# Last output tile in two passes over half the tokens, y laid out by halves, and 18 instead of 12 first products

## The chip, the cores and the metric

The kernel runs on one core of a Trainium2 chip. The metric is the device time of one execution in microseconds, from the median of the runs shown. The engines are called as in the profile: PE is TensorE's products, PEld its weight loads (they overlap the products), DVE is VectorE, ACT ScalarE, POOL GpSimd, SP SyncE, which here only issues DMAs.

## The reference, cut to what matters

One inference step of a hybrid decoder with two layers, for 256 prompt tokens and 8 sample tokens, model width 1024, f32. Each layer is a mixer with residual, then a feed-forward part with residual:

```python
def conv_ffn(x, prev, norm_g, w_gate, w_up, conv_w, conv_b, w_down):
    T = x.shape[1]
    h = rmsnorm(x, norm_g)
    g = h @ w_gate
    g_all = jnp.concatenate([prev, g], axis=1)
    gc = sum(conv_w[i] * g_all[:, i:i + T] for i in range(CONV_W)) + conv_b
    a = jax.nn.gelu(gc) * (h @ w_up)
    return x + a @ w_down, g_all[:, -(CONV_W - 1):]
...
y_prompt = rmsnorm(xp, final_norm)
y_sample = rmsnorm(xs, final_norm)
```

The change sits at the very end: `a @ w_down` of layer 1 (2816 to 1024), the residual, and the final RMSNorm, which needs the sum of squares over all 1024 channels of a token before any channel of that token can be scaled. It also touches the very beginning, where products of ones keep TensorE busy until the first data arrive.

## The kernel before, in words

All 264 tokens are columns: activations lie with 128 channels on the partitions and the T = 264 tokens along the row. X, the residual stream, is a tile of 128 x 8 x 264, one slice m of 264 columns for each 128 channels.

Weights are packed on the host into blocks of 128 x 128 in exactly the order in which TensorE uses them. They come from memory in chunks of 8 or 16 blocks (`raw`, issued on SP's queue), and `split` turns 8 blocks at a time into a high part `wh` (ScalarE, L299, rounded to fp32r) and a low part `wl` (VectorE, L300, the remainder). Activations have the same two parts. A block therefore costs three products, all with a moving operand of 128 x 264: high weights times high activations, high times low, low times high, each with a weight load of its own. `run` goes over an order of (output tile m, block k), adds into one PSUM bank for each m, and calls `evac(m, o)` after the last block of m. In the down projection `dn1` there are 8 output tiles of 22 blocks (NF = 22), 66 products each.

`residual(..., operand=False, R=R)` gives the evac of `dn1`: z = PSUM times R of the feed-forward norm (L579), X += z (L581), the square of X (`Norm.add`, L397 on ScalarE; the squares of tiles 0 to 6 are summed into `acc_fin` on GpSimd, that of tile 7 stays apart), and X times the gain of the final norm (L586). `Norm.finish` then multiplies `acc_fin` and the last square by a matrix of ones on TensorE (`ns_fin`, ordinary fp32, two rows in the profile for each product), which sums over the partitions; Ln and Exp on ScalarE (L421, L422) make `R_fin`. The last loop (L1093 to L1096) scales X in five pieces on VectorE and stores each, on SP's and ScalarE's queue in turn:

```python
    for i, (m, e) in enumerate(YD):
        x = X[:, m:e, :]
        v.tensor_tensor(x, x, R.unsqueeze(1).to_broadcast([P, e - m, T]), ALU.mult)
        (s if i % 2 else nc.sync).dma_start(a["y"][m:e].rearrange("m p t -> p m t"), x)
```

At the beginning, WARM = 12 bf16 products of a tile of ones (128 x 256, `warm`) run before the first real product (L372, L373).

The order on each engine is made by a scheduler when the program is built, except where `keep_in_program_order` pins it: `fixed[0]` pins TensorE's products in the mixers, and the weight DMAs are pinned on SP.

Of the kernel before, what the change touches and what calls it, by code (L numbers as in the profile page):

```python
# [9 lines left out]
F32 = mybir.dt.float32  # L10
# [3 lines left out]
AF = mybir.ActivationFunctionType  # L14
ALU = mybir.AluOpType
# [3 lines left out]
P = 128  # L19
D = 1024  # L20
KD = D // P
SEQ = 256
NS = 8
T = SEQ + NS
# [7 lines left out]
NF = DFF // P  # L32
# [2 lines left out]

MMB = 4
KQ = 5
WARM = 12
YD = ((0, 1), (1, 3), (3, 5), (5, 7), (7, 8))

NEG = -1e30
SCALE = HD ** -0.5
# [108 lines left out]
def _consts():  # L151
# [41 lines left out]
    ("sguw", (P, 512)), ("sgub", (P, 512)), ("poolw", (P, 512)),  # L193
]
_OUTS = [
    ("y", (KD, P, T)), ("k0", (P, 4, T)), ("v0", (P, 4, T)), ("bvn", (P, 4, NS)),
    ("k1", (P, 4, T)), ("v1", (P, 4, T)), ("poolp", (P, 4, NST)), ("pools", (P, 4, NS, 16)),
    ("cv0", (P, NF, 10)), ("cv1", (P, NF, 10)), ("cs0", (P, NF, NS)), ("cs1", (P, NF, NS)),
]
# [3 lines left out]
def tile_decoder_step(ctx: ExitStack, tc: tile.TileContext, a):  # L203
    nc = tc.nc
    v, s, g = nc.vector, nc.scalar, nc.gpsimd
    fixed = [False]
# [13 lines left out]
    pe = TensorE()  # L220
# [6 lines left out]
    sm = ctx.enter_context(tc.tile_pool(name="sm", bufs=3))  # L227
# [3 lines left out]
    def f4(name, shape=(P, 4, T), dt=F32):  # L231
        return up.tile(list(shape), dt, tag="u", name=name)

    def mv(name):
        return [f4(f"{name}_{x}", dt=F32R) for x in "hl"]

    def hl(tiles, k):
        return tiles[k // 4][0][:, k % 4, :], tiles[k // 4][1][:, k % 4, :]

    def at(name):  # L240
        return psa.tile([P, 512], F32, tag="at", name=name)

    X = con.tile([P, KD, T], F32, name="X")
# [7 lines left out]
    def mmb(name):  # L251

        return psm.tile([P, 512], F32, tag="mm", name=name)

    def vec(n):
        o, w = _VEC[n]
        return VEC[:, o:o + w]
# [18 lines left out]
    def wtiles(tt):  # L276
        return [wsp.tile([P, 8 * P], F32R, tag=f"w{x}", name=f"w{x}{tt}") for x in "hl"]

    def raw(ci):
        if ci not in raws:  # L280
            n = _CHUNKS[ci] * P
            r = f4(f"raw{ci}", (P, n)) if ci < C8 else rawp.tile([P, n], F32, tag="raw", name=f"raw{ci}")
            o = (coff[ci] - 16) * P * P
            raws[ci] = r
            late(r, a["w"][o:o + P * n].rearrange("(p f) -> p f", p=P))
        return raws[ci]

    LOOK = 3
    pos = [0]

    def split(t):
        for tt in range(len(splits), min(t + (2 if t == 3 else LOOK), NT - 1) + 1):
            ci = chunk_of[tt]
            for c in range(ci, min(ci + 3, len(_CHUNKS))):
                raw(c)
            o = (tt * 8 - coff[ci]) * P
            src = raws[ci][:, o:o + 8 * P]
            h, l = splits[tt] = wtiles(tt)
            s.activation(h, src, AF.Copy)  # L299
            v.tensor_tensor(l, src, h.bitcast(F32), ALU.subtract)  # L300
        return splits[t]

    spare = (32, 40)

    def run(order, rhs, evac, hooks=None):
        hooks = sorted((hooks or {}).items())
        n = 0
        seen, left, ps = {}, {}, {}
        for m, k in order:
            left[m] = left.get(m, 0) + 1  # L310
        for m, k in order:
            i = pos[0]
            pos[0] += 1
            h, l = split(i // 8)
            c = (i % 8) * P
            if m not in ps:
                ps[m] = at(f"mm{i}") if i in spare else psm.tile([P, 512], F32, tag="mm", name=f"mm{i}")
                first = True
            else:
                first = False  # L320
            left[m] -= 1
            o = ps[m][:, :T]
            xh, xl = rhs(m, k)
            pe.matmul(o, h[:, c:c + P], xh, start=first, stop=False)
            pe.matmul(o, h[:, c:c + P], xl, start=False, stop=False)
            pe.matmul(o, l[:, c:c + P], xh, start=False, stop=left[m] == 0)
            if left[m] == 0:
                evac(m, o)
            n += 1
            while hooks and n >= round(8 * (hooks[0][0] + 1)):  # L330
                for f in hooks.pop(0)[1]:
                    f()

    orders = dict(_PHASES)
# [9 lines left out]
    first, o = [], 0  # L344
    for i in range(len(_FIRST)):
        g_, w_, x_ = _first_cols(i)
        n = g_ + w_ + x_
        r = f4(f"xw{i}", (P, n))
# [22 lines left out]
    pw = at("warm")  # L371
    for i in range(WARM):  # L372
        tc.keep_in_program_order(pe.matmul(pw[:, :256], warm[:, :P], warm, start=i == 0, stop=i == WARM - 1))  # L373

    ident = cst("ident")
    ones = con.tile([P, P], F32, name="ones")
    v.memset(ones, 1.0)
    epst = con.tile([P, 1], F32, name="epst")
# [11 lines left out]
    class Norm:  # L390
        def __init__(self, name, two=False):
            self.name, self.two, self.last = name, two, []
            self.acc = None

        def add(self, m, src=None):
            q = sm.tile([P, T], F32, tag="sq", name=f"sq_{self.name}{m}")
            i = s.activation(q, X[:, m, :] if src is None else src, AF.Square)  # L397
            if src is not None:
                tc.keep_in_program_order(i)
            if m == KD - 1 and self.two:  # L400
                self.last.append(q)
            elif self.acc is None:
                self.acc = q
            elif m == 1:
                n = sm.tile([P, T], F32, tag="acc", name=f"acc_{self.name}", bufs=2)
                g.tensor_tensor(n, self.acc, q, ALU.add)
                self.acc = n
            else:
                g.tensor_tensor(self.acc, self.acc, q, ALU.add)
# [1 line left out]
        def finish(self, pin=False):  # L411
            return rstd_of([self.acc] + self.last, 1.0 / D, self.name, pin)

    def rstd_of(parts, scale, name, pin=False, bank=None):
        p = (bank or at)(f"ns_{name}")
        for i, x in enumerate(parts):
            mm = pe.matmul(p[:, :T], ones, x, start=i == 0, stop=i == len(parts) - 1)
            if pin:
                tc.keep_in_program_order(mm)
        R = sm.tile([P, T], F32, tag="R", name=f"R_{name}", bufs=2)  # L420
        s.activation(R, p[:, :T], AF.Ln, bias=epst, scale=scale)  # L421
        last[0] = s.activation(R, R, AF.Exp, scale=-0.5)  # L422
        return R

# [111 lines left out]
        g.tensor_tensor(C0[:, l], C0[:, l], t, ALU.add)  # L536
        nc.sync.dma_start(a[f"cs{l}"], CSTATE[:, l, 1])

    def ffn(l, xg, R, down_evac, hooks=None):
        cw, cb = vec("cw"), vec("cb")  # L540
        wc = lambda i, j: cw[:, (l * 3 + i) * NF + j:(l * 3 + i) * NF + j + 1]
        cvo = sm.tile([P, NF, 10], F32, tag="cvo", name=f"cvo{l}", bufs=1)
        act = [mv(f"a{l}_{i}") for i in range((NF + 3) // 4)]
        half = {}

        def evac(m, o):
            n, j = m
            if n == "g":
                wk = f4(f"wk{l}_{j}", (P, 2, T))
                C = wk[:, 0, :]  # L550
                G = wk[:, 1, :]
                v.tensor_tensor(G, o, R, ALU.mult)  # L552
                s.activation(C, G, AF.Identity, scale=wc(2, j), bias=cb[:, l * NF + j:l * NF + j + 1])
                v.scalar_tensor_tensor(C[:, 1:SEQ], G[:, 0:SEQ - 1], wc(1, j), C[:, 1:SEQ], ALU.mult, ALU.add)
                v.scalar_tensor_tensor(C[:, 2:SEQ], G[:, 0:SEQ - 2], wc(0, j), C[:, 2:SEQ], ALU.mult, ALU.add)
                v.tensor_tensor(C[:, SEQ:T], C[:, SEQ:T], C0[:, l, j, :], ALU.add)
                s.activation(cvo[:, j, :], G[:, SEQ - 2:T], AF.Copy)
                s.activation(C, C, AF.Gelu_apprx_tanh)
                half[j] = wk
            else:  # L560
                wk = half.pop(j)
                C, A = wk[:, 0, :], wk[:, 1, :]
                v.tensor_tensor(A, o, C, ALU.mult)
                halves(*hl(act, j), A)

        run(orders[f"ff{l}"], lambda m, k: hl(xg, k), evac)
        nc.sync.dma_start(a[f"cv{l}"], cvo)
        lnexp()
        run(orders[f"dn{l}"], lambda m, k: hl(act, k), down_evac, hooks)

    def residual(gain, name, operand=True, R=None):
        xg = [mv(f"xg_{name}{i}") for i in range(2)] if operand else None
# [23 lines left out]
    xg = [mv(f"xg_0{i}") for i in range(2)]  # L596
    nrm = Norm("n0", True)
# [307 lines left out]
    xg, nrm, evac = residual(vec("f0"), "f0")  # L905
    run(orders["out0"], pick([catA, catB]), evac, hk)
    fixed[0] = False
    R = nrm.finish()
    gelu_set()
    xg1, nrm1, evac = residual(vec("n1"), "n1", R=R)  # L910
# [9 lines left out]
    xg = xg1  # L920
# [164 lines left out]
    xg, nrm, evac = residual(vec("f1"), "f1")  # L1085
    run(orders["out1"], pick([catA, catB]), evac, hk)
    fixed[0] = False
    R = nrm.finish()
    gelu_set()
    _, nrm, evac = residual(vec("fin"), "fin", operand=False, R=R)  # L1090
    ffn(1, xg, R, evac)
    R = nrm.finish()
    for i, (m, e) in enumerate(YD):  # L1093
        x = X[:, m:e, :]
        v.tensor_tensor(x, x, R.unsqueeze(1).to_broadcast([P, e - m, T]), ALU.mult)  # L1095
        (s if i % 2 else nc.sync).dma_start(a["y"][m:e].rearrange("m p t -> p m t"), x)  # L1096


def _lay(inp):
# [66 lines left out]
```

## Time and profile before

| what | value |
|---|---|
| median of 3 runs | 603.81 us (603.23 to 604.20) |
| the profiled execution, device time | 605.38 us |
| its span in the profile | 603.6 us |
| granted TensorE clock over the span | 0.997 |
| PE, DVE, ACT busy | 590.4, 424.7, 339.9 us |
| last product of the last output tile starts | 593.72 us |
| last y scaling ends | 599.85 us |

The span lacks the 1.8 us that lie around it in the device time. In the timeline a row is: start in us, length in us, engine, line, operation, output from inputs, shapes, how many instructions were merged into the row, and in brackets the idle time of the engine before it with what ended it. In groups, the numbers behind the bar are total us and mean ns of one instruction. A product's length includes a drain that overlaps the next product, so a stream's cost is read from start to start. "a" is the feed-forward activation (high and low part), "mm" a PSUM accumulator of the trunk, "half" in the changed kernel one of half the tokens.

### The profile page before, as it was taken

Reading aid. Unit: us, or ns where it says so; the run is one execution under the profiler, and the core shown is the slowest. Engines: PE = TensorE matmul, PEld = TensorE weight load, DVE = VectorE, ACT = ScalarE, POOL = GpSimd, SP = SyncE. Lnnn points to the kernel's source line nnn. Section 1 sums busy time; section 2 is a strip of 40 time slices with the busy share of each in tenths; the row PEclk is TensorE's granted clock in tenths of the full one; section 3 lists DMA queues with packets and bytes.
Section 4 is the critical chain, followed back from the end, with each engine's and each line's share of the span. In section 5 each row is a group of like instructions: output and inputs, shape, how many; then the busy total and the mean of one; then the engine's idle time right before and its main releaser. Section 6 shows DMA issues by size and latency. Waiting matters only on the chain.

```text
span 603.6 us, 12258 instructions
## 1 busy us (share of the span) xinstructions
PE 590.4 (98%) x4900; PEld 571.4 (95%) x4900; DVE 424.7 (70%) x745; ACT 339.9 (56%) x597; POOL 42.8 (7%) x59
## 2 busy tenths in 40 slices
PE   8989999999999999999999999999999999999994
PEld 7988879999999999999999878999999999999993
DVE  6899565958878778576569676686877777755542
ACT  7557754656555656454454466656665555555431
POOL 4101002300000000001120000030000000001210
PEclk9999999999999999999999999999999999999998
DMA  8998845454554645796466763554545545455402
GB/s 310 352 378 328 272 153 205 155 204 149 201 176 174 208 150 201 260 370 212 151 251 248 262 206 113 173 205 148 208 149 201 179 171 207 152 208 171 179 1 72
DMA packets 28090, 122.39 MB, mean 203 GB/s; under 512 B 3330, under 2 KB 5250, under 8 KB 16642
## 3 DMA queue, kind: packets, MB, share of 16 engines
q1 hardware_dynamic: 27200, 120.42, 56.4%
q10 hardware_dynamic: 834, 1.20, 0.6%
q8 instruction: 38, 0.62, 0.4%
q14 instruction: 18, 0.15, 0.1%
HBM read 117.65 MB, written 3.96 MB: 201 GB/s over the span
## 4 chain that ended last, share of the span: by engine, by line
PE 91%; DVE 2%; DMA 2%; SPq 2%; ACT 2%; issue 1%; ACTq 0%; DVEq 0%
PE mm L215 83%; DMA raw<-in_w 1%; PE pv_l L215 1%; PE sc L215 1%; SPq L340 1%; PE pav L215 1%; PE pt L218 1%; DVE wl L300 1%; DMA PT<-in_pt 1%; ACT wh L299 1%; PE S L215 1%; PE Z L215 1%; SPq L274 0%; PE pf L215 0%; DVE X L1095 0%
## 5 line engine op out<-in xcount | busy, mean ns | idle before, releaser
L299 ACT ACTIVATE wh<-raw 128x1024 fp32r<-128x1024 f32 x179 | 189.6, 1062 | 198.6 <-PE mm L215 185.1
L300 DVE TENSOR_TENSOR wl<-raw,wh 128x1024 fp32r<-128x1024 f32 x179 | 219.1, 1225 | 112.5 <-ACT wh L299 111.5
L215 PE MATMUL mm<-xg_f_h,wh 128*128 128x264 f32 x704 | 200.6, 285 | 0.3 <-DVE wk L552 0.3
L215 PE MATMUL mm<-xg_f_l,wh 128*128 128x264 f32 x704 | 199.9, 284 | 0.0
L215 PE MATMUL mm<-xg_f_h,wl 128*128 128x264 f32 x704 | 198.6, 282 | 0.0
L215 PEld LDWEIGHTS mm<-xg_f_h,wh 128*128 128x128 f32 x704 | 132.2, 188 | 0.8 <-issue 0.7
L215 PEld LDWEIGHTS mm<-xg_f_l,wh 128*128 128x128 f32 x704 | 132.3, 188 | 0.1
L215 PEld LDWEIGHTS mm<-xg_f_h,wl 128*128 128x128 f32 x704 | 132.2, 188 | 0.0
L215 PE MATMUL mm<-a_h,wh 128*128 128x264 f32 x352 | 99.9, 284 | 0.0
L215 PE MATMUL mm<-a_l,wh 128*128 128x264 f32 x352 | 99.8, 284 | 0.0
L215 PE MATMUL mm<-a_h,wl 128*128 128x264 f32 x352 | 99.3, 282 | 0.0
L215 PEld LDWEIGHTS mm<-a_l,wh 128*128 128x128 f32 x352 | 66.1, 188 | 0.0
L215 PEld LDWEIGHTS mm<-a_h,wh 128*128 128x128 f32 x352 | 66.1, 188 | 0.0
L215 PEld LDWEIGHTS mm<-a_h,wl 128*128 128x128 f32 x352 | 66.1, 188 | 0.0
L215 PE MATMUL mm<-xg_h,wh 128*128 128x264 f32 x160 | 48.2, 302 | 1.1 <-ACT xg_h L384 1.1
L215 PE MATMUL mm<-xg_l,wh 128*128 128x264 f32 x160 | 46.2, 289 | 0.0
L215 PE MATMUL mm<-xg_h,wl 128*128 128x264 f32 x160 | 46.1, 288 | 0.0
L215 PE MATMUL mm<-xg_n_h,wh 128*128 128x264 f32 x128 | 38.6, 302 | 0.0
L215 PE MATMUL mm<-xg_n_l,wh 128*128 128x264 f32 x128 | 36.3, 283 | 0.0
L215 PE MATMUL mm<-xg_n_h,wl 128*128 128x264 f32 x128 | 36.2, 283 | 0.0
L215 PEld LDWEIGHTS mm<-xg_h,wh 128*128 128x128 f32 x160 | 30.8, 193 | 4.4 <-issue 2.7
L215 PEld LDWEIGHTS mm<-xg_l,wh 128*128 128x128 f32 x160 | 30.8, 193 | 0.3 <-DVE xg_l L385 0.2
(237 smaller groups left out, 842.4 us busy)
## 6 DMA issues: line engine op xcount, KB each, us to landing
raw<-in_w SPq DMA_DIRECT2D x89, 1024.0 KB, 4.8
K<-in_kt SPq DMA_DIRECT2D x32, 256.0 KB, 6.5
V<-in_vp SPq DMA_DIRECT2D x32, 256.0 KB, 5.6
raw<-in_w SPq DMA_DIRECT2D x4, 512.0 KB, 5.9
X<-in_x SPq DMA_DIRECT2D x4, 264.0 KB, 7.8
xw<-in_xw SPq DMA_DIRECT2D x2, 388.0 KB, 5.4
out_k<-k SPq DMA_DIRECT2D x1, 528.0 KB
out_v<-v SPq DMA_DIRECT2D x1, 528.0 KB, 4.9
```

Of the source, the lines that this page charges most:

```text
L215: return self.keep(nc.tensor.matmul(*x, **k))
L218: return self.keep(nc.tensor.transpose(*x, **k))
L299: s.activation(h, src, AF.Copy)
L300: v.tensor_tensor(l, src, h.bitcast(F32), ALU.subtract)
L340: regs.append(nc.sync.value_load(PT[0:1, i:i + 1], min_val=0, max_val=NPHYS - 1))
```

## The change

- The last output tile of `dn1` (m = 7) is done by `last_tile` in two passes of 66 products each, over tokens 0 to 131 and 132 to 263 (HT = 132). Each pass has a PSUM bank of its own. The weights of all 22 blocks are split ahead and used by both passes.
- After each pass, its half is evacuated (`tail`): z, the add into X, the square (`add_half`), the gain. The rest for that half (`rest`: norm product, Ln, Exp, scalings, stores) is emitted for the first half behind block 12 of the second pass (AT = 12), for the second half after the pass. TensorE's order is pinned from there on.
- y is laid out as 2 halves of (128 partitions, 8 slices, 132 tokens), with three scalings and stores for the first half and four for the second. The host puts it back.
- WARM is 18.

```diff
-WARM = 12
-YD = ((0, 1), (1, 3), (3, 5), (5, 7), (7, 8))
+WARM = 18
+HT = T // 2
+YD = (((0, 2), (2, 5), (5, 8)), ((0, 1), (1, 3), (3, 6), (6, 8)))
...
-    ("y", (KD, P, T)), ...
+    ("y", (2, P, KD, HT)), ...
...
+    AT = 12
+    def last_tile(order, rhs, evac):
+        blocks = []
+        for m, k in order:
+            i = pos[0]
+            pos[0] += 1
+            h, l = split(i // 8)
+            blocks.append((h[:, i % 8 * P:(i % 8 + 1) * P], l[:, i % 8 * P:(i % 8 + 1) * P], k))
+        todo = None
+        for r in range(2):
+            o = mmb(f"half{r}")[:, :HT]
+            c = slice(r * HT, (r + 1) * HT)
+            for n, (h, l, k) in enumerate(blocks):
+                xh, xl = rhs(m, k)
+                pe.matmul(o, h, xh[:, c], start=n == 0, stop=False)
+                pe.matmul(o, h, xl[:, c], start=False, stop=False)
+                pe.matmul(o, l, xh[:, c], start=False, stop=n == len(blocks) - 1)
+                if r and n == AT:
+                    todo()
+            todo = evac(m, o, c, r)
+        todo()
...
-        run(orders[f"dn{l}"], lambda m, k: hl(act, k), down_evac, hooks)
+        dn = orders[f"dn{l}"]
+        if not l:
+            run(dn, lambda m, k: hl(act, k), down_evac, hooks)
+            return
+        run(dn[:-NF], lambda m, k: hl(act, k), down_evac, hooks)
+        fixed[0] = True
+        last_tile(dn[-NF:], lambda m, k: hl(act, k), tail)
...
-    ffn(1, xg, R, evac)
-    R = nrm.finish()
-    for i, (m, e) in enumerate(YD):
-        x = X[:, m:e, :]
-        v.tensor_tensor(x, x, R.unsqueeze(1).to_broadcast([P, e - m, T]), ALU.mult)
-        (s if i % 2 else nc.sync).dma_start(a["y"][m:e].rearrange("m p t -> p m t"), x)
+    def tail(m, o, c, r):
+        m = m[1]
+        z = sm.tile([P, HT], F32, tag="zh", name=f"zh{r}", bufs=2)
+        v.tensor_tensor(z, o, R[:, c], ALU.mult)
+        v.tensor_tensor(X[:, m, c], X[:, m, c], z, ALU.add)
+        q = nrm.add_half(m, c, r)
+        s.activation(X[:, m, c], X[:, m, c], AF.Copy, scale=vec("fin")[:, m:m + 1])
+        def rest():
+            Rh = rstd_of([nrm.acc[:, c], q], 1.0 / D, f"fin{r}", n=HT)
+            for i, (b, e) in enumerate(YD[r]):
+                x = X[:, b:e, c]
+                v.tensor_tensor(x, x, Rh.unsqueeze(1).to_broadcast([P, e - b, HT]), ALU.mult)
+                (s if i % 2 else nc.sync).dma_start(a["y"][r, :, b:e, :], x)
+        return rest
+    ffn(1, xg, R, evac, tail=tail)
```

`add_half` squares X[:, m, c] into a tile of 132 columns; `rstd_of` takes the width n. Up to the last tile, and apart from the six added products at the start, every engine's order is that of before. What moves stands at the end of the program, in three places.

TensorE (PE) before, the end: the last two blocks of tile 7, 264 columns wide, then the norm product.

```order
L215 MATMUL mm_7415<-a_5_h,wh_7374 128x264
L215 MATMUL mm_7415<-a_5_l,wh_7374 128x264
L215 MATMUL mm_7415<-a_5_h,wl_7375 128x264
L215 MATMUL ns_fin<-acc_fin,ones 128x264
L215 MATMUL ns_fin<-sq_fin_7485,ones 128x264
```

PE after, around block 12 of the second pass (half_7494 is the second half's accumulator, half_7421 the first's):

```order
L216 MATMUL half_7494<-a_3_h,wh_7352 128x132
L216 MATMUL half_7494<-a_3_l,wh_7352 128x132
L216 MATMUL half_7494<-a_3_h,wl_7353 128x132
L216 MATMUL ns_fin_7534<-acc_fin,ones 128x132
L216 MATMUL ns_fin_7534<-sqh_fin_7491,ones 128x132
L216 MATMUL half_7494<-a_3_h,wh_7352 128x132
L216 MATMUL half_7494<-a_3_l,wh_7352 128x132
L216 MATMUL half_7494<-a_3_h,wl_7353 128x132
```

The first half's norm product stands inside the second pass, with 9 blocks of that pass behind it; the second half's stands last, where the only one stood before.

VectorE (DVE) before, from the last evacuation to the end:

```order
L579 TENSOR_TENSOR z_fin_7482<-mm_7415,R_f_5226 128x264
L581 TENSOR_TENSOR X<-X,z_fin_7482 128x264
L1095 TENSOR_TENSOR X<-X,R_fin 128x264
L1095 TENSOR_TENSOR X<-X,R_fin 128x528 x3
L1095 TENSOR_TENSOR X<-X,R_fin 128x264
```

DVE after:

```order
L1130 TENSOR_TENSOR zh_7488<-half_7421,R_f_5232 128x132
L1131 TENSOR_TENSOR X<-X,zh_7488 128x132
L1139 TENSOR_TENSOR X<-X,R_fin_7537 128x2x132
L1139 TENSOR_TENSOR X<-X,R_fin_7537 128x3x132 x2
L1130 TENSOR_TENSOR zh_7573<-half_7494,R_f_5232 128x132
L1131 TENSOR_TENSOR X<-X,zh_7573 128x132
L1139 TENSOR_TENSOR X<-X,R_fin_7582 128x132
L1139 TENSOR_TENSOR X<-X,R_fin_7582 128x2x132
L1139 TENSOR_TENSOR X<-X,R_fin_7582 128x3x132
L1139 TENSOR_TENSOR X<-X,R_fin_7582 128x2x132
```

The first half's three scalings stand ahead of the second half's evacuation, and behind that evacuation are four scalings of 1056 columns in all, where five of 2112 were.

ScalarE (ACT) before, the same stretch:

```order
L397 ACTIVATE sq_fin_7485<-X 128x264
L586 ACTIVATE X<-X,VEC 128x264
L421 ACTIVATE R_fin<-ns_fin,epst 128x264
L422 ACTIVATE R_fin<-R_fin 128x264
L1096 DMA out_y<-X 128x2x264 x2
```

ACT after:

```order
L421 ACTIVATE sqh_fin_7491<-X 128x132
L1133 ACTIVATE X<-X,VEC 128x132
L450 ACTIVATE R_fin_7537<-ns_fin_7534,epst 128x132
L451 ACTIVATE R_fin_7537<-R_fin_7537 128x132
L1140 DMA out_y<-X 128x3x132
L421 ACTIVATE sqh_fin_7576<-X 128x132
L1133 ACTIVATE X<-X,VEC 128x132
L450 ACTIVATE R_fin_7582<-ns_fin_7579,epst 128x132
L451 ACTIVATE R_fin_7582<-R_fin_7582 128x132
L1140 DMA out_y<-X 128x2x132 x2
```

ScalarE's chain stands twice, at half width, and a store of the first half is issued on its queue ahead of the second half's square.

More of the change, by code (lines that the diff above doesn't have):

```diff
@@ L195 @@
 _OUTS = [
-    ("y", (KD, P, T)), ("k0", (P, 4, T)), ("v0", (P, 4, T)), ("bvn", (P, 4, NS)),
+    ("y", (2, P, KD, HT)), ("k0", (P, 4, T)), ("v0", (P, 4, T)), ("bvn", (P, 4, NS)),
     ("k1", (P, 4, T)), ("v1", (P, 4, T)), ("poolp", (P, 4, NST)), ("pools", (P, 4, NS, 16)),
@@ L393, in __init__, with add_half @@
             self.acc = None
+        def add_half(self, m, c, r):
+            q = sm.tile([P, HT], F32, tag="sqh", name=f"sqh_{self.name}{r}", bufs=2)
+            s.activation(q, X[:, m, c], AF.Square)
+            return q
         def add(self, m, src=None):
@@ L412, in finish, with rstd_of @@
             return rstd_of([self.acc] + self.last, 1.0 / D, self.name, pin)
-    def rstd_of(parts, scale, name, pin=False, bank=None):
+    def rstd_of(parts, scale, name, pin=False, bank=None, n=T):
         p = (bank or at)(f"ns_{name}")
         for i, x in enumerate(parts):
-            mm = pe.matmul(p[:, :T], ones, x, start=i == 0, stop=i == len(parts) - 1)
+            mm = pe.matmul(p[:, :n], ones, x, start=i == 0, stop=i == len(parts) - 1)
             if pin:
                 tc.keep_in_program_order(mm)
-        R = sm.tile([P, T], F32, tag="R", name=f"R_{name}", bufs=2)
-        s.activation(R, p[:, :T], AF.Ln, bias=epst, scale=scale)
+        R = sm.tile([P, n], F32, tag="R" if n == T else "Rh", name=f"R_{name}", bufs=2)
+        s.activation(R, p[:, :n], AF.Ln, bias=epst, scale=scale)
         last[0] = s.activation(R, R, AF.Exp, scale=-0.5)
@@ L537, in conv_prep, with ffn @@
         nc.sync.dma_start(a[f"cs{l}"], CSTATE[:, l, 1])
-    def ffn(l, xg, R, down_evac, hooks=None):
+    def ffn(l, xg, R, down_evac, hooks=None, tail=None):
         cw, cb = vec("cw"), vec("cb")
@@ L1145 @@
     o = {n: np.asarray(r.results[0]["out_" + n]) for n, _ in _OUTS}
-    y = o["y"].transpose(2, 0, 1).reshape(T, D)
+    y = o["y"].transpose(0, 3, 2, 1).reshape(T, D)
     def kv(k, w):
```

## Prediction

> **What bounds the kernel.** I read the page's busy shares and its chain first, then the chain and the timeline of the last 18 us, then the weight loads by shape, since the change halves the width of products and so doubles their number, and last the first 42 us.
>
> ```profile
> PE 590.4 (98%) x4900; PEld 571.4 (95%) x4900; DVE 424.7 (70%) x745; ACT 339.9 (56%) x597; POOL 42.8 (7%) x59
> PE 91%; DVE 2%; DMA 2%; SPq 2%; ACT 2%; issue 1%; ACTq 0%; DVEq 0%
> ```
>
> TensorE is the bound (98% busy, 91% of the chain), so a product that is added inside the stream is paid in full. Only the two ends of the span hold anything else. The end, by the chain (start, us, what) and by the timeline:
>
> ```profile
> 585.84 0.28 PE L215 MATMUL mm<-a_h,wh 128*128 128x264 f32 x1
> ...
> 593.72 0.28 PE L215 MATMUL mm<-a_h,wl 128*128 128x264 f32 x1
> 593.84 0.60 PE L215 MATMUL ns_fin<-acc_fin,ones 128*128 128x264 f32 x2
> ...
> 595.50 0.71 PE L215 MATMUL ns_fin<-sq_fin,ones 128*128 128x264 f32 x2 [1.06 <-ACT sq_fin L397]
> ...
> 597.22 2.63 DVE L1095 TENSOR_TENSOR X<-X,R_fin 128x264 f32<-128x264 f32 x5 [2.28 <-ACT R_fin L422]
> ```
> ```profile
> 594.03 0.44 DVE z_fin L579
> ...
> 594.50 0.44 DVE X L581
> ...
> 595.03 0.43 ACT sq_fin L397
> ...
> 595.50 0.73 PE ns_fin L215 x2
> ...
> 596.25 0.49 ACT R_fin L421
> ...
> 596.77 0.43 ACT R_fin L422
> ```
>
> The last tile's 66 products (22 blocks, three each) start from 585.84 to 593.72: 7.88 us over 65 steps, 121 ns a step. Behind the last of them everything is serial: z, the add into X, the square, the norm product, Ln, Exp, five scalings of y until 597.22 + 2.63 = 599.85, then the last store and the closing, 603.6 - 599.85 = 3.75 us. From the last product's start to the end that is 9.9 us, the part that the change shortens.
>
> **The second pass.** It replaces 66 products of 264 columns by 132 of 132 columns. Per product one weight load of 128x128 remains. So the question is the step of a narrow product: half of 121 ns, or what a weight load takes.
>
> ```profile
> L215 PEld LDWEIGHTS pv_l<-V,PZ 128*32 128x32 f32 x64 | 1.7, 109 | 3.0 <-issue 2.5
> L215 PEld LDWEIGHTS pav<-pT,vt 128*64 128x64 f32 x64 | 4.7, 136 | 0.8 <-issue 0.2
> L215 PEld LDWEIGHTS mm<-a_h,wh 128*128 128x128 f32 x352 | 66.1, 188 | 0.0
> ```
> ```profile
> 73.19 0.30 PEld L215 LDWEIGHTS pO<-ow,CST 128*128 128x128 f32 x2
> 73.29 0.31 PE L215 MATMUL pO<-ow,CST 128*128 128x32 f32 x2
> 81.11 1.31 PEld L215 LDWEIGHTS pf<-sguc,vgt 128*128 128x128 f32 x11
> ```
>
> The first three rows are groups by shape (total us, mean ns of one), the others the timeline (start, length). A load lasts 109, 136 and 188 ns for 32, 64 and 128 columns: 0.81 to 0.84 ns a column, so 128 columns occupy the loader for 104 to 108 ns, and some 82 ns of the 188 are latency that overlaps. Loads that follow each other bear it out: eleven pf loads take 1.31 us, (1.31 - 0.19)/10 = 112 ns apart, and pO's two loads, under products only 32 columns wide that cannot hide anything, stand 0.30 - 0.19 = 0.11 us apart. At 264 columns the load hides under the stream; at 132 the stream should need about 60 ns, and the load is what the next product waits for. No row shows a narrow product of the fp32r kind of the trunk. The ends for its step are 60.6 ns (half of 121, load fully hidden) and 121 ns (nothing gained by narrowing); nearest is the load-bound row, and I take 112 ns.
>
> [...]
>
> The first half's norm product now stands inside the second pass, behind block 12. Its two fp32 products make two rows each on TensorE (593.84, x2 above), four rows of at least a load, 4 x 0.112 = 0.45. Behind fp32 rows the next trunk product starts late:
>
> ```profile
> 83.17 0.37 PE L215 MATMUL mm<-xg_h,wh 128*128 128x264 f32 x1
> 83.38 0.28 PE L215 MATMUL mm<-xg_l,wh 128*128 128x264 f32 x1
> ```
>
> 0.21 us instead of 0.12, another 0.09: 0.54 in all. It waits for the first half's square on ScalarE, and the rest of the pass stands behind it; but 39 products, 39 x 0.112 = 4.4 us, run first, against 0.3 + 0.44 + 0.44 + 0.43 us of drain, z, add and square at full width. No wait there. The first half's Ln, Exp, three scalings and three store issues (two on SP's queue, one on ACT's, ahead of the second half's square) need under 3 us more, and end about when the 8 us pass does; nothing of them is on the path unless the pass is much shorter.
>
> Last product starts at 585.84 + 131 x 0.112 + 0.54 = 601.05 instead of 593.72: **+7.33 us**.
>
> **The shorter end.** The second half carries 132 columns through the same chain.
>
> ```profile
> L1095 DVE TENSOR_TENSOR X<-X,R_fin 128x528 f32<-128x528 f32 x3 | 1.9, 701 | 0.0
> L1095 DVE TENSOR_TENSOR X<-X,R_fin 128x264 f32<-128x264 f32 x2 | 0.9, 429 | 2.3 <-ACT R_fin L422 2.3
> L950 ACT ACTIVATE keep<-Z 128x255 f32<-128x255 f32 x8 | 3.2, 398 | 0.0
> L950 ACT ACTIVATE keep<-Z 128x127 f32<-128x127 f32 x8 | 2.3, 287 | 1.9 <-issue 1.1 <-PE Z L215 0.8
> ```
>
> VectorE: (701 - 429)/264 = 1.03 ns a column, 0.136 us for 132, for z and the add: -0.27. ScalarE: 111 ns for 128 columns, so about 0.11 each for square, Ln and Exp: -0.33. The norm product: its second row starts 0.60 - 0.38 = 0.22 us behind the first, 264 columns; half of it, in two rows: -0.22. The last product's own stream: -0.06. The y scalings: 2112 columns in five cost 2.63 = 2112 x 1.03 ns + 5 x 0.09; 1056 in four cost 1.09 + 0.36 = 1.45: -1.18. The stores:
>
> ```profile
> out_y<-X ACTq DMA_DIRECT2D x2, 264.0 KB, 2.6
> out_y<-X SPq DMA_DIRECT2D x2, 132.0 KB, 2.2
> ```
>
> The last store is 132 KB as before (two times 132 tokens), with half the bytes ahead of it, so it can land 0 to 0.4 us earlier (2.6 against 2.2); I take -0.2. SP and ACT issue one more store between them, each beside a scaling. Together **-2.26 us**. Layout of y by halves: packets of 1056 to 1584 bytes instead of 1056, nothing in the sum.
>
> **The 18 first products.**
>
> ```profile
> 1.20 2.74 PE L215 MATMUL warm<-warm 128*128 128x256 bf16 x12 [1.20 <-DVE warm L370]
> 5.05 0.59 PE L215 MATMUL mm<-xg_h,wh 128*128 128x264 f32 x1 [1.11 <-ACT xg_h L384]
> 8.93 0.28 PE L215 MATMUL mm<-xg_h,wh 128*128 128x264 f32 x1
> 18.25 0.33 SPq L274 DMA_DIRECT2D raw<-in_w  x1
> 26.16 1.06 ACT L299 ACTIVATE wh<-raw 128x1024 fp32r<-128x1024 f32 x1 [2.61 <-DMA raw<-in_w]
> 30.93 2.96 ACT L299 ACTIVATE wh<-raw 128x1024 fp32r<-128x1024 f32 x3
> 32.02 1.23 DVE L300 TENSOR_TENSOR wl<-raw,wh 128x1024 fp32r<-128x1024 f32 x1 [0.97 <-ACT wh L299]
> ```
> ```profile
> PE S L215 <- DVE k L676: 2.0, 1, 2.0
> ```
>
> Twelve take 2.74 us, about 0.21 a step; six more end near 1.20 + 18 x 0.21 = 5.0, just when the first real product's operand is ready (5.05). They may bring full speed (rows of 0.28 us, from 8.93) earlier. Either way the effect is covered: before 40.5 us TensorE waits 2.0 us for k from VectorE, and that follows ScalarE's split at 30.93, which hangs behind the weights that SP asked for at 18.25 and that ended ScalarE's wait at 26.16. None of that waits for TensorE. Up to 2 us of gain or loss ends in this wait: 0. If the cover were gone, the gain could be what half-speed steps cost from 5.05 to 8.93, at most 1.9 us.
>
> **Sum.** +7.33 - 2.26 + 0 = +5.1 us. The profiled execution took 605.38 us, which would become 610.5; it lies 1.6 above the median of the runs, 603.81, from which the forecast is 608.9.
>
> **Rivals.**
> Narrow products take half a step (load hidden after all): 131 x 0.0606 + 0.54 - 7.88 - 2.26 = -1.7 us, 602.1, faster. It decides from a step of 73 ns, (7.88 + 2.26 - 0.54)/131. For it speaks only that loads overlap products at 264 columns; against it the 112 ns of pf and the 0.11 of pO. [...]
>
> An intermediate step, load and stream partly overlapped, as long as two thirds of 121 ns (81): 10.6 + 0.54 - 7.88 - 2.26 = +1.0, 604.8, no change that can be told. The rows at 112 ns speak against it. [...]
>
> Narrow products run like fp32, two rows each (pO: one product of 32 columns, x2 rows): 131 x 0.224 + 0.54 - 7.88 - 2.26 = +19.7, 623.5. Against it: the trunk's 264 wide products make one row and one load each (704 and 704 in the same group); for it only that no trunk product under 264 columns is on record.
>
> The front does give something: at most -1.9 on any case. Held off by the wait at 40.5; it changes no sign of the first case.
>
> **Numbers.** Load-bound 0.80, half step 0.09, intermediate 0.04, two rows 0.07. In the first case the step runs from 108 to 121 ns (+4.5 to +6.3), and the end saves 1.8 to 2.8 us (its columns' prices a fifth to a quarter off, the last landing 0 to 0.4), so +4.0 to +6.7; with half a us for the spread of the runs that is 607.2 to 611.0, rounded outward to 607.0, which leaves out 2 in 10. A measurement can tell about 0.2%, 1.2 us. Faster 0.09, same 0.04, slower 0.87.
>
> **What would show it.** In the timeline after, half products 0.11 to 0.12 us apart with a load of 188 ns between each, and the last of them starting near 601; 0.06 apart would prove me wrong at once, 0.22 and doubled rows as well. z to Exp some 0.8 us shorter, the scalings near 1.45 us, the stores of the first half landed before the last product. The wait for k before 40.5 us longer by whatever the front gains. If the norm product inside the second pass waits for ScalarE, a step of mine is wrong.

## The result, and the profile after

| | us | ratio to before, 95% interval |
|---|---|---|
| before, median of 4 runs | 603.61 (603.23 to 604.20) | 1 |
| changed kernel, median of 4 runs | 609.62 (609.51 to 613.10) | 1.0108 (1.0089 to 1.0126) |

The change makes the kernel slower by 6.0 us between the medians; the lower end of the interval is 5.4 us. The changed kernel's profiled execution took 609.51 us, its span 607.7.

The chain that ended last, over the last tile (start, us, what):

```profile
584.66 11.67 PE half L216 x105
596.34 0.50 PE ns_fin L216 x4
596.84 2.98 PE half L216 x27
...
599.84 0.31 DVE zh L1130
...
600.17 0.31 DVE X L1131
...
600.50 0.32 ACT sqh_fin L421
...
600.87 0.51 PE ns_fin L216 x2
...
601.40 0.38 ACT R_fin L450
...
601.80 0.32 ACT R_fin L451
```

The timeline inside the first pass, and the scalings at the end:

```profile
591.71 0.27 PE L216 MATMUL half<-a_h,wl 128*128 128x132 f32 x1
591.82 0.28 PE L216 MATMUL half<-a_h,wh 128*128 128x132 f32 x1
591.93 0.27 PE L216 MATMUL half<-a_l,wh 128*128 128x132 f32 x1
592.04 0.28 PE L216 MATMUL half<-a_h,wl 128*128 128x132 f32 x1
...
602.14 1.47 DVE L1139 TENSOR_TENSOR X<-X,R_fin 128x132 f32<-128x132 f32 x4 [1.68 <-ACT R_fin L451]
```

Half as many columns, and the products still start 0.11 us apart; 105 products and the start of a norm product fill 11.67 us, 111 ns each. Before, the stretch from the last tile's first product (585.84) to the end of the span took 17.8 us; now it takes 607.7 - 584.5 = 23.2: +5.4. Of that the stream is +7.15 (from 7.88 to 15.03 between the first and the last product's start), and the end behind the last product -1.73 (from 9.89 to 8.16).

The last tile's first product comes 1.3 us earlier than in the profile of before, which looks like a gain of the 18 first products. It is none, as the first experiment shows: two executions of the same front differ by nearly as much (584.50 here, 585.61 there).

The weight loads of the half products, one for each product and about as long as before (188 ns):

```profile
L216 PEld LDWEIGHTS half<-a_h,wl x44: 191/192/192, 584.6 to 599.5; 128*128 128x128 f32 x44
L216 PE MATMUL half<-a_h,wl x44: 272/274/278, 584.7 to 599.5; 128*128 128x132 f32 x44
```

(shortest, median, longest in ns; first and last start.) A product 132 columns wide lasts 274 ns, hardly less than one of 264 columns (282). Its load's row starts 0.06 us ahead of it (591.87 and 591.93) and lasts 0.19 us, so it seems to start and then wait for its weights. The run with loads of 64 columns tests this.

### The profile page after: what moved, and what is told of

It reads as the page before. It is cut to its first block, busy times and chain, and to the rows that moved or that the text cites. A ratio compares the mean times of both kernels' runs of the same rounds, so it can differ in the third digit from the quotient of the medians.

```text
span 607.7 us, 12419 instructions
## 1 busy us (share of the span) xinstructions
PE 597.6 (98%) x4976; PEld 578.5 (95%) x4976; DVE 425.0 (70%) x749; ACT 340.8 (56%) x601; POOL 43.4 (7%) x59
## 2 busy tenths in 40 slices
DMA packets 29147, 122.41 MB, mean 201 GB/s; under 512 B 3362, under 2 KB 6306, under 8 KB 17698
## 4 chain that ended last, share of the span: by engine, by line
PE 91%; DVE 3%; DMA 2%; issue 1%; SPq 1%; ACT 1%; ACTq 0%; DVEq 0%
PE mm L216 81%; PE half L216 2%; DMA raw<-in_w 1%; PE pv_l L216 1%; DVE wl L302 1%; PE sc L216 1%; PE pav L216 1%; PE pt L219 1%; DMA PT<-in_pt 1%; PE S L216 1%; SPq L364 1%; PE Z L216 1%; ACT wh L301 1%; PE pf L216 0%; PE pm L216 0%
## 5 line engine op out<-in xcount | busy, mean ns | idle before, releaser
L216 PE MATMUL mm<-a_h,wh 128*128 128x264 f32 x330 | 93.6, 284 | 0.0
L216 PE MATMUL mm<-a_l,wh 128*128 128x264 f32 x330 | 93.5, 284 | 0.0
L216 PE MATMUL mm<-a_h,wl 128*128 128x264 f32 x330 | 93.1, 282 | 0.0
L216 PEld LDWEIGHTS mm<-a_l,wh 128*128 128x128 f32 x330 | 62.0, 188 | 0.0
L216 PEld LDWEIGHTS mm<-a_h,wh 128*128 128x128 f32 x330 | 62.0, 188 | 0.0
L216 PEld LDWEIGHTS mm<-a_h,wl 128*128 128x128 f32 x330 | 62.0, 188 | 0.0
L216 PEld LDWEIGHTS mm<-xg_h,wl 128*128 128x128 f32 x160 | 30.1, 188 | 1.1 <-DVE wl L650 1.0
```

Of the source, the lines that this page charges most:

```text
L216: return self.keep(nc.tensor.matmul(*x, **k))
```

## The experiments

All of them start from the changed kernel or from the one before, and each ratio is to runs of the kernel before on the same chip. Theory: a narrow product's step is the time of its weight load, so the second pass costs 66 loads; the 18 first products change nothing. Rivals: the step has another cause, or the front takes part.

**The 18 first products alone.**

```diff
-WARM = 12
+WARM = 18
```

> The kernel before with 18 first products instead of 12, nothing else. Theory (the wait for k before 41 us takes whatever the front gains or loses): no change, 603.6 within 0.6 us, and in the trace the clock opens earlier than 8.9 us while that wait grows or follows the landing of the weights. Rival 1 (the front gains, since the changed kernel's last tile starts at 584.50 instead of 585.84 in the two profiles): 602.3. Rival 2 (the six products cost something, which would explain why the medians lie 6.0 apart and the two ends of the profiles only 5.4): 604.2.

Measured: 604.41 against 604.05 us, 1.0011 (0.9999 to 1.0023), 11 and 21 runs. From its timeline and its waits:

```profile
4.90 0.59 PE L215 MATMUL mm<-xg_h,wh 128*128 128x264 f32 x1
...
6.00 0.29 PE L215 MATMUL mm<-xg_h,wh 128*128 128x264 f32 x1
```
```profile
PE S L215 <- DVE k L676: 1.9, 1, 1.9
PE mm L215 <- DVE wl L615: 0.6, 1, 0.6
```

The products come in rows of 0.28 to 0.29 us from 6.00 us on, those of before from 8.93, where its clock record has the full clock begin (8.91). That the six products bring this is not shown: with 12 of them the next experiment begins its last tile 0.2 us behind the changed kernel (584.82 and 584.66 in the chains) and the last experiment 0.65 us ahead of it (584.01), while before, with 12 too, begins it 1.3 us behind. The earlier short rows put this run 1.2 us ahead of before at its 13th real product (7.09 against 8.28 us). By 17.5 us only 0.2 of that is left; 0.6 went into a wait for a weight split that was not there before. So the gain ends ahead of the wait for k, which is 2.0 us in the profile of before and 1.9 here, but 0.8 in the changed kernel and 0.9 in the next experiment, which has 12 first products. The product that waits for k, before and in the changed kernel:

```profile
40.49 0.49 PE L215 MATMUL S<-k,q 64*128 64x128 f32 x4 [2.04 <-DVE k L676]
```
```profile
39.20 0.49 PE L216 MATMUL S<-k,q 64*128 64x128 f32 x4 [0.80 <-DVE k L711]
```

From its start to the last tile's first product it takes 545.3 us in each of the ten profiles that have this wait, with 12 first products and with 18. So the 1.3 us are the difference between these two starts. The weights that SP asks for at about 18.2 us landed at 26.1 in the profile of before, 7.8 us after the request, and at 23.3 in the changed kernel, 4.9 us after it, in the order of the two starts; that they alone set it is not shown. The rival that the front gains 1.3 us has fallen; no change and a cost of 0.6 us both lie inside the interval (-0.1 to 1.4 us), so the theory holds as far as this run can tell.

**The passes alone.** The changed kernel with WARM = 12.

> The changed kernel with 12 first products: the two passes and the layout of y alone. Theory: the passes carry the whole change, 609.6 within 0.6 us (ratio 1.009 to 1.011), half products 111 to 113 ns apart. Rival (18 products gain 1.3 us that the passes give away again): 610.9. Rival (the 18 products cost 0.6): 609.0.

Measured: 609.34 us, 1.0089 (1.0075 to 1.0102), that is +4.5 to +6.2 us. From the first product of the last tile to the end its profile takes 22.9 us, +5.2 over before. The passes are the change.

**Loads of 64 columns.** As many half products, as wide, but with half the weight columns:

```diff
-                pe.matmul(o, h, xh[:, c], start=n == 0, stop=False)
+                pe.matmul(o[:64], h[:, :64], xh[:, c], start=n == 0, stop=False)
```

(and likewise the other two products of a block, z and the add.)

> As the passes alone, but each half product loads only 64 of the 128 weight columns and makes 64 rows of output; the other 64 output channels of the last tile get no feed-forward term (part of the computation left out). As many products, as wide, but loads of 64 columns, 52 to 54 ns instead of 104 to 108. Theory (the load sets the step): the step falls to that of the stream of 132 columns or of the load, 55 to 62 ns, and the last product starts 131 x 0.052 = 6.8 us earlier: about 602.8 us. Rival (narrow fp32r products have a step of 112 ns for another reason, such as a fixed price per product): no change against the passes alone, 609.6.

Measured: 603.50 us, 0.999 (0.9981 to 1.0), 5.8 us below the passes alone. Chain, and the load and product groups:

```profile
584.69 6.48 PE half L216 x105
```
```profile
L216 PEld LDWEIGHTS half<-a_h,wl x44: 133/135/139, 584.6 to 593.0; 128*64 128x64 f32 x44
L216 PE MATMUL half<-a_h,wl x44: 222/225/228, 584.6 to 593.1; 128*64 128x132 f32 x44
```

The 105 products that took 11.67 us take 6.48, 62 ns each, with nothing changed in them but the loads and, with these, the rows of output: 192 ns of load became 135, and 274 ns of product 225. So the load sets the step of the narrow product here; the stream of 132 columns alone allows 62 ns or less. Columns of weights and rows of output cannot be told apart by this run; for the load speaks that its own row became 57 ns shorter and the step 49. This also prices the forecast's rival: with a hidden load the passes would have ended about level with before (0 to 1.1 us ahead of it here), not 1.7 us ahead, because the first half's scalings (1.40 us from 592.45, in the chain) then collide with the second half's evacuation, which starts at 593.8, 0.7 us behind the last product, and the stores cost more than I took. Whether the 62 ns are the load's of 64 columns or the stream's is not shown.

**Cut at token 200.** A first pass 200 wide, a second 64 wide.

```diff
-HT = T // 2
+CUT = (0, 200, T)
...
+            c = slice(CUT[r], CUT[r + 1])
+            o = mmb(f"half{r}")[:, :CUT[r + 1] - CUT[r]]
```

> As the passes alone (12 first products), but cut at token 200: a first pass 200 wide, a second 64 wide; y laid out to match. Theory (the weight load sets the step of every product narrower than about 250 columns): 112 ns a step in both passes, so the passes cost as much as with 132 and 132; the second half's chain has 68 columns less (z and add 0.14, three ScalarE steps 0.18, norm product 0.1, scalings 0.55): 0.9 us less than the passes alone, about 608.7. Rival (a fixed price per product beside a stream of half a ns a column): steps of about 140 and 85 ns, sum as before. Rival (stream sets the step): 92 and 30 ns, the sum of the passes 8 us, total near 602.

Measured: 612.63 us, 1.0139 (1.0122 to 1.0156): 3.3 us above the passes alone instead of 0.9 below. By windows (length, busy us of each engine, granted clock, DMA share, GB/s) and in the timeline of the second pass:

```profile
584.10:591.40 7.30, 7.30 (x68) 7.30 (x67) 0.87 (x2) 0.94 (x2) 0.76 (x1) 1.00 0.01 2
591.50:594.20 2.70, 2.70 (x28) 2.70 (x26) 0.73 (x2) 0.83 (x2) 0.00 (x0) 1.00 0.00 0
594.30:604.00 9.70, 9.70 (x45) 9.70 (x45) 1.97 (x3) 0.80 (x2) 0.00 (x0) 0.50 0.26 84
```
```profile
593.85 0.28 PE L216 MATMUL half<-a_l,wh 128*128 128x64 f32 x1
593.97 0.28 PE L216 MATMUL half<-a_h,wl 128*128 128x64 f32 x1
594.08 0.28 PE L216 MATMUL half<-a_h,wh 128*128 128x64 f32 x1
594.19 0.38 PE L216 MATMUL half<-a_l,wh 128*128 128x64 f32 x1
594.38 0.40 PE L216 MATMUL half<-a_h,wl 128*128 128x64 f32 x1
594.59 0.40 PE L216 MATMUL half<-a_h,wh 128*128 128x64 f32 x1
```

The step is as the theory says at first: 0.11 us, with 200 columns (66 products in 7.3 us) and with 64. Then, 2.7 us into the narrow pass, the granted clock falls from 1.00 to 0.50 and the step from 0.11 to 0.21 us, though TensorE is busy by its rows all the time. That was no part of the expectation. Some 45 rows of products are left by then, each 0.1 us longer from start to start, about 4.5 us by this estimate, which covers the 3.9 us that the run lies above the 608.7 expected.

**Three passes of 88 tokens.** To see whether the width does that.

```diff
-HT = T // 2
+HT = T // 3
...
-        for r in range(2):
+        for r in range(3):
```

> The passes alone (12 first products) with three passes of 88 tokens instead of two of 132. Theory (each pass costs 66 loads, whatever its width): another 66 x 0.112 = 7.4 us and a norm product of 0.45, less 0.6 for a last chain of 88 columns: 7.2 over the two passes, about 616.5, if the clock holds. With 64 columns in a step of 112 ns (29 us of stream in 112) the clock was halved 2.8 us into the pass, with 132 it held for 15 us. If 88 columns (a third of the step) are too few as well, most of the 22 us runs at 213 ns a step: 630 to 637. Rival (the clock fell in the run with 64 columns for a cause outside the width): 616.5.

Measured: 633.16 us, 1.0496 (1.0476 to 1.0515).

```profile
584.70:590.00 5.30, 5.30 (x50) 5.30 (x49) 0.86 (x2) 0.94 (x2) 0.75 (x1) 1.00 0.00 0
590.20:604.00 13.80, 13.80 (x67) 13.80 (x67) 0.72 (x3) 1.26 (x4) 0.00 (x0) 0.50 0.00 1
604.00:623.00 19.00, 19.00 (x91) 19.00 (x91) 2.33 (x8) 1.25 (x4) 0.00 (x0) 0.50 0.15 39
```

The same for the passes alone, with 132 columns:

```profile
584.70:592.00 7.30, 7.30 (x69) 7.30 (x67) 0.87 (x2) 0.94 (x2) 0.75 (x1) 1.00 0.01 2
592.00:599.70 7.70, 7.70 (x72) 7.70 (x70) 1.99 (x5) 1.40 (x4) 0.00 (x0) 1.00 0.06 17
```

The clock falls with 88 columns too, 5.5 us into the first narrow pass, and stays down to the end. With 132 columns a step it held through 15 us. So in these runs the clock fell with 88 columns at a step of 0.11 us (50 products in 5.30 us) and held with 132; nothing between them was tried.

**One pass, the end by halves.** The first half's norm, scalings and stores can overlap with the second half's without any second load: the last tile runs in one pass, and both halves are evacuated behind it.

```diff
+        o = mmb("last")
+        for n, (h, l, k) in enumerate(blocks):
+            xh, xl = rhs(m, k)
+            pe.matmul(o[:, :T], h, xh, start=n == 0, stop=False)
+            pe.matmul(o[:, :T], h, xl, start=False, stop=False)
+            pe.matmul(o[:, :T], l, xh, start=False, stop=n == len(blocks) - 1)
+        todo = [evac(m, o[:, r * HT:(r + 1) * HT], slice(r * HT, (r + 1) * HT), r) for r in range(2)]
+        for f in todo:
+            f()
```

(The order on VectorE and ScalarE is pinned too, and the first half's stores all go on SP's queue.)

> 12 first products; the last tile in one pass of 66 products 264 wide as before, and only what follows is done by halves: z, add and square of both halves, then norm product, Ln, Exp, scalings and stores of the first half while the second half's norm runs (order pinned on VectorE and ScalarE; y by halves). No weight is loaded twice. Theory (the second pass of loads is the whole loss): the 5 us are gone, and the first scaling starts about 2.8 us after the last product's start instead of 3.5, the last ends at about 5.7 instead of 6.1: 603.2 to 604.0, 0 to 0.5 us below before. Rival (the end by halves costs by itself, through more stores and seven scalings instead of five): 604.5 or more.

Measured: 605.15 us, 1.0026 (1.0014 to 1.0039). The rival was right: the second pass's 5 us are gone, but the end costs by itself. The last scaling ends 5.4 us behind the last product's start (6.1 before, 5.7 expected); behind it the stores need 5.6 us instead of 3.75. From its DMA table over the end, and from before's:

```profile
DMA packets 2160, 1.08 MB, mean 132 GB/s; under 512 B 112, under 2 KB 2160, under 8 KB 2160
out_y<-X ACTq DMA_DIRECT2D x2, 132.0 KB, 4.1
```
```profile
DMA packets 1104, 1.08 MB, mean 208 GB/s; under 512 B 80, under 2 KB 1104, under 8 KB 1104
```

(The mean GB/s are over windows of 8.2 and 5.2 us, so they cannot be compared.) The same 1.08 MB goes in twice as many packets. A half of a slice of X is 132 tokens, 528 bytes, and 2048 packets of that size (the 2160 less the 112 under 512 bytes) make up the 1.08 MB, though y is laid out by halves in memory.

**The end by halves, GpSimd scaling two slices of each half.**

```diff
-                v.tensor_tensor(x, x, Rh.unsqueeze(1).to_broadcast([P, e - b, HT]), ALU.mult)
+                (g if b == 6 else v).tensor_tensor(x, x, Rh.unsqueeze(1).to_broadcast([P, e - b, HT]), ALU.mult)
```

(The pieces of each half are chosen so that slices 6 and 7 are one piece.)

> As the one pass with halves, but GpSimd scales slices 6 and 7 of each half beside VectorE's six. If GpSimd takes about 1 us for 264 columns beside VectorE (its sums of 264 columns took 0.76 alone and 1.4 beside VectorE), the last scaling ends 0.5 us earlier: about 602.9 to 603.5. Rival (both engines slow each other, or the store waits for GpSimd): 603.8 or more.

Measured: 606.05 us, 1.0037 (1.0023 to 1.005), no better than without GpSimd. VectorE's five scalings take longer than its seven did:

```profile
595.85 3.17 DVE L1148 TENSOR_TENSOR X<-X,R_fin 128x396 f32<-128x396 f32 x5 [1.14 <-ACT R_fin L449]
595.90 2.15 POOL L1148 TENSOR_TENSOR X<-X,R_fin 128x264 f32<-128x264 f32 x2 [8.02 <-ACT R_fin L449]
```
```profile
594.75 2.77 DVE L1148 TENSOR_TENSOR X<-X,R_fin 128x264 f32<-128x264 f32 x7 [1.14 <-ACT R_fin L449]
```

(with GpSimd; without.) 3.17 us instead of 2.77 with a quarter less to do. At the forecast's 1.03 ns a column and 0.09 us a scaling, which make 2.8 us of the seven, the five would take 2.1 us by this estimate: side by side with GpSimd, VectorE was 1.1 us slower. What GpSimd's scalings would take alone was not measured.

**Packed stores, with the passes and with one pass.** The scalings write into a tile in which a partition's slices of one half lie side by side.

```diff
+            YT = f4(f"yt{r}", (P, KD, HT))
             for i, (b, e) in enumerate(YD[r]):
-                x = X[:, b:e, c]
-                v.tensor_tensor(x, x, Rh.unsqueeze(1).to_broadcast([P, e - b, HT]), ALU.mult)
+                x = YT[:, b:e, :]
+                v.tensor_tensor(x, X[:, b:e, c], Rh.unsqueeze(1).to_broadcast([P, e - b, HT]), ALU.mult)
```

> The passes alone (12 first products), but the scaled halves go into a tile of their own in which a partition's slices lie side by side, so that a store's packets are 528 bytes for each slice put together (528 to 1584 bytes, 1056 for the last store) instead of 528 bytes each. Theory (the packets of 528 bytes, since half a slice of X is 132 tokens, are what held the last store): the last store lands 2.2 to 2.4 us after its issue instead of 2.63 and 2.87, total 0.2 to 0.5 us below the passes alone, ratio about 1.008. Rival (the landing hangs on the queue or the number of stores): no change, 1.009.

Measured: 608.48 us, 1.0076 (1.0062 to 1.009); in its profile 22.3 us from the last tile's first product to the end, against 22.9 without packing. By its DMA table the last two stores, on ScalarE's queue, land 1.9 us after their issue (median), where the changed kernel's take 2.4. In the times the gain is not clear of noise: this interval and that of the passes alone (1.0075 to 1.0102) overlap.

> The one pass with the end by halves, with the scaled halves in a packed tile in the same way. With packets of 528 bytes the stores, 1.08 MB from 595.2 to 602.0 us, were what ended last: the last took 4.4 us from issue to landing, and the run was 0.26% slower than before. Theory (packet size): 1.08 MB at the 350 GB/s that packets of 1056 bytes reached before, last landing 2.5 to 2.9 us after issue, the end 1.5 us earlier: ratio 0.9985 to 1.0005, the only form with a chance to be below before. Rival (seven stores, five of them on one queue, set the end): unchanged, 1.0025.

Measured: 602.71 us, 0.9982 (0.9972 to 0.9992), 11 and 15 runs. In its DMA table over the end:

```profile
DMA packets 1008, 1.08 MB, mean 180 GB/s; under 512 B 112, under 2 KB 1008, under 8 KB 1008
out_y<-yt ACTq DMA_DIRECT2D x2, 132.0 KB, 2.2
```

The last stores, on ScalarE's queue, land 2.2 us after issue instead of 4.1. From the last tile's first product to the end it takes 600.6 - 583.85 = 16.75 us, 1.0 less than before. The stores are as many as without packing and on the same queues, and the seven scalings take 2.77 us in both, so the rival has fallen: what differs is the packed tile, and with it the packets, 1008 instead of 2160 for the same bytes. This form, with 12 first products, is the only complete one below before: by 1.1 us (0.5 to 1.7).

## Why the prediction was right

The kernel was forecast at 608.9 us and took 609.62, inside the range, by the mechanism that the forecast put first. One of its four runs, 613.10, lies above the range.

The step of the narrow product: forecast 112 ns from the spacing of other weight loads, measured 111 to 112, and put down to the load by the run with 64 weight columns. The stream from the first to the last product: forecast 15.2 us, measured 15.0. The norm product inside the second pass waits for nothing, and its four rows took 0.50 us in the chain.

The chain from the last product's start to the first scaling: forecast 0.88 us shorter, measured 0.89 (3.50 to 2.61). The scalings: forecast 1.45, measured 1.47.

The term that was mis-sized is the stores. I put the packets at "1056 to 1584 bytes instead of 1056, nothing in the sum" and took the landing 0.2 us earlier. The page of the profile after counts 29147 packets instead of 28090 for the same bytes: they are 528 bytes. From the last scaling's end to the end of the span it takes 4.08 us instead of 3.75, +0.33 instead of -0.2 (3.84 in the profile of the passes alone, so the term was 0.3 to 0.5 us too low). I looked at how y lies in memory and not at how a half of X lies on the chip. The stream came out 0.2 us shorter than forecast, so the two errors partly cancel, by luck: the sum over the last tile is +5.4 instead of +5.1. Packed stores gave about 0.7 us back by the profiles.

The front: forecast 0, measured 1.0011 (0.9999 to 1.0023). The value fits, but the wait that the forecast named is not what covers it: the profiled gain of 1.2 us was all but gone by 17.5 us, before the wait for k. That wait varied from nothing to 2.0 us between the eleven profiles, which the one profile of before could not show.

Two signs that the forecast named did not come. The wait for k became shorter, not longer (0.8 us). And the first half's stores had not landed when the last product started at 599.53: the last of them was issued at 599.09 and landed at 602.52. In this profile that cost nothing that shows: their bytes had moved by 601.3, before the second half's first store was issued at 602.46.

What stays open: the medians lie 6.0 us apart, the two profiled ends 5.4. The intervals, 5.4 to 7.6 for the changed kernel and 4.5 to 6.2 with 12 first products, hold both; whether the 18 products cost a few tenths was not settled.

## What to carry to other kernels

In these runs a product had a floor that its width did not lower: the load of its weights, 112 ns for 128 columns, so a narrower product paid for a stream that it did not have: 64, 132 and 200 columns all had this step at full clock, 264 one of 121 ns. Cutting the tokens in two doubled the loads, from 66 to 132, that the step of 121 ns had hidden. Before splitting a pass, compare the columns of the weights with those of the operand; if only what follows is to overlap, split that and leave the products whole. And where a tile is cut, look at the runs that it leaves on both sides of a store: in the one-pass form, stores in runs of 528 bytes landed 1.9 us later after their issue than packed ones.

## What was not expected of the hardware

The granted clock fell to half under a TensorE that was never idle by its rows: 2.7 us into a stream of 64 columns each 112 ns, 5.5 us into one of 88, and not in 15 us of 132. The runs with 88 and 132 columns have the same loads and the same step, so up to the fall they differ in the columns streamed in a step alone; how these act on the clock is not shown. Nor do 2.7 and 5.5 us say how long the clock holds: each is from one profile, and what sets the moment of the fall is not shown.

Three passes took 23.8 us more than two. The third pass was expected to cost 7.2 us at full clock; the other 16.6 us are, by this estimate, what the halved clock cost.
